# The second-last projection of a hybrid encoder layer: sixteen output columns one by one, or eight pairs by seven products with weight sums prepared earlier

## The chip, the cores and the metric

The kernel runs on one core of a Trainium2 chip. The metric is the device time of one execution in microseconds (us), lower is better. The core's engines run side by side and wait for each other through semaphores: TensorE (PE in the profile, its weight loads PEld), VectorE (DVE), ScalarE (ACT), GpSimd (POOL) and SyncE (SP), which here issues all the DMA transfers, from one queue, in order.

## The reference

One layer, 512 prompt tokens and 8x16 decode tokens, which the kernel handles as one block of T = 640 tokens, D = 2048:

```python
z = x @ w_in                                  # q, k, v, gates, merge gates
y_a = (fox_attention(q, k, v) * silu(gate_a)) @ w_out_fox
y_b = (rms_norm(gated_delta(...)) * silu(gate_b)) @ w_out_gdn
h = (sigmoid(m_a) * y_a + sigmoid(m_b) * y_b) @ w_out
x1 = layer_norm(DEEPNORM_ALPHA * x + h, ln_g, ln_b)
e = rms_norm(p_l @ w_pl_proj, pl_norm_w)
x_out = x1 + sigmoid(x1 @ w_pl_gate) * e
```

All in float32. The decode tokens' attention also reads a cache of 512 past rows for each of 8 heads. The change concerns `@ w_out` and what prepares it.

## The kernel before

**Products.** Every operand of a large product is split into a high and a low part (`xh`, `xl` of the activations; `wh`, `wl` of the weights): ACT casts the high part, DVE subtracts it from the source. Three matmuls (high by high, high by low, low by high) then stand for one product. Activations lie transposed, 16 tiles `k` of 128 features by 640 tokens, each in two halves of 320 tokens. One output column is 128 features: 16 steps `s`, each with 2 halves x 3 = 6 matmuls of 128x320, 96 in all, made by `column` (L319 and L320 in the profile). Its weights are two halves of 128x1024 (`wr`, three buffers, 512 KB each), cast in four pieces of 128x512 (L265 ACT, L266 DVE), up to five pieces ahead of their use (`w_ahead`; `plan` writes the list of halves and pieces).

**Pairs.** In the front, 14 pairs of columns go by seven products in place of eight (`pair`, L394): the 2x2 blocks (feature halves by column) of the weights are added and subtracted into seven combinations, the two token halves' activations into seven forms (X11, X21, X22, T1 to T4), and each product is 8 `k` by 3 matmuls. Sums of the products give both columns. There, the weight sums (b, S1, S2, S3) are made on DVE just ahead of their use (L255).

**Stages in order of time.** The front (input split, value columns, pairs) ends at about 505 us. Attention (`phase_fox`) follows to about 845 us: eight heads, each with a q and a k column of main matmuls, and between these the head's own work (scores, biases L622/L688, softmax L572 to L577, products with v) with loads of the k and v cache (`kc`, `vc`, four of 512 KB each). Then come the gated delta rule, w_out_fox, and `tail`: w_out_gdn to about 1778 us (eight double columns, each ending in `gated`, L1551 and L1554, which merges the branches into the tiles `mg`), w_out to about 2004 us (16 columns; L1625 adds `xr`, the input, giving the tile `r`; `moments`, L1588 to L1596, sums r and its square for the layer norm), and w_pl_gate on the split of r (`gsplit`, L305) to the end.

**What sets the order.** Nothing is scheduled by a compiler: the program's own order is each engine's order. Main matmuls are the beat; after every second step `tick` lets side work advance. Side work is generators in lanes (`work`, `conv`, ...), which yield the number of ticks to wait for (one tick is 0.88 us by the planner's clock); a dry lane may go on at every tick, the others at every second one and only with a free PSUM bank. The planner keeps an estimated clock of PE, DVE, ACT and POOL (`saw`), by which a positive yield also waits for the engines' work; it has none for DMA. `until(cond)` runs ticks with no matmuls until a condition holds.

**Tail.** The split of `mg[0..7]` stands in the w_out_gdn columns, of 8 to 11 in the last one's second half, of 12 to 15 in the first w_out column. `r[0..6]` are split in the last w_out column, the others in the first w_pl_gate column:

```python
            def after(s):
                if n == 15 and s >= 2 and s % 2 == 0:
                    gsplit(s // 2 - 1)
```

Tiles have their own names and buffers (`ld`, `m`, `re`, ...), and all 16 tiles r stay in SBUF.

## Time and profile before

| what | value |
|---|---|
| median of 3 runs | 2245.84 us (2243.6 to 2247.39) |
| the profiled execution's own time | 2244.35 us |
| its span | 2242.6 us |
| PE busy | 2230.1 us, 99% |
| DVE, ACT, POOL busy | 1332.7, 842.2, 68.5 us |
| granted TensorE clock | 0.999 |
| DMA | 304.56 MB, 136 GB/s over the span |

Times are microseconds from the start of the profiled span. The execution's own time has 1.75 us around the span. "L266" is line 266 of the program; `out<-in` names what an instruction writes and reads; "idle before, releaser" is the time the engine waited and for what. A DMA's "us to landing" counts from its issue on SP.

### The profile page before, as it was taken

The page shows a single profiled execution, that of the slowest core. Times are in us where ns is not written, and L with a number is a line of the kernel's source. Part 1 is how long each engine was busy: PE and PEld are TensorE (multiplying, and loading weights), DVE is VectorE, ACT ScalarE, POOL GpSimd, SP SyncE. Part 2 cuts the span into 40 slices and gives each one's busy share as a digit, 9 for nine tenths or more (in the row PEclk, how much of TensorE's full clock was granted, in tenths as well). Part 3 has the DMA queues.
Part 4 walks back from the last instruction along what each step waited for, and adds up shares of the span by engine and source line. Part 5 has one row for each costly group of instructions (what it writes and reads, how often), then busy time and mean ns, then how long its engine had stood idle before and what let it go on. Part 6 is the DMA issues. An engine that isn't in the chain of part 4 may idle for free.

```text
span 2242.6 us, 40023 instructions
## 1 busy us (share of the span) xinstructions
PE 2230.1 (99%) x15938; PEld 2160.2 (96%) x15938; DVE 1332.7 (59%) x2831; ACT 842.2 (38%) x1874; POOL 68.5 (3%) x230
## 2 busy tenths in 40 slices
PE   9999999999999999999999999999999999999999
PEld 7889999999999999999999999999999999999999
DVE  5476766663444445476686676686446534667555
ACT  4244444443333344443443543544332212242222
POOL 0000000000000000000000000000000000020000
PEclk9999999999999999999999999999999999999999
DMA  6333333238665634232332332335446522323332
GB/s 235 119 120 118 105 117 126 99 128 289 210 229 202 231 130 145 93 106 84 108 107 84 117 102 89 110 122 178 148 170 231 175 99 84 105 94 118 115 120 70
DMA packets 118378, 304.56 MB, mean 136 GB/s; under 512 B 22680, under 2 KB 30952, under 8 KB 118192
## 3 DMA queue, kind: packets, MB, share of 16 engines
q1 hardware_dynamic: 118192, 302.01, 40.3%
q8 instruction: 125, 2.05, 0.4%
q14 instruction: 61, 0.50, 0.1%
HBM read 250.15 MB, written 51.82 MB: 135 GB/s over the span
## 4 chain that ended last, share of the span: by engine, by line
PE 96%; DMA 2%; DVE 1%; ACT 0%; issue 0%; SPq 0%; DVEq 0%; ACTq 0%
PE g L319 34%; PE g L320 34%; PE g L394 15%; PE g L363 4%; PE s L363 1%; PE s L699 1%; DMA wr<-in_w 1%; PE s L657 1%; PE s L858 1%; PE s L616 1%; PE s L995 1%; DMA kc<-in_kc 0%; PE s L715 0%; PE s L1082 0%; PE s L1072 0%; PE s L1067 0%
## 5 line engine op out<-in xcount | busy, mean ns | idle before, releaser
L266 DVE TENSOR_TENSOR wl<-wr,wh 128x512 fp32r<-128x512 f32 x556 | 380.8, 690 | 523.2 <-ACT wh L265 516.3
L265 ACT CAST wh<-wr 128x512 fp32r<-128x512 f32 x556 | 342.5, 620 | 623.1 <-PE g L320 506.9
L319 PE MATMUL g<-xh,wh 128*128 128x320 f32 (+1 forms) x1712 | 549.6, 321 | 1.2 <-ACT wh L265 1.2
L319 PE MATMUL g<-xl,wh 128*128 128x320 f32 (+1 forms) x1712 | 529.9, 310 | 0.3 <-DVE xl L294 0.2
L320 PE MATMUL g<-xh,wh 128*128 128x320 f32 x1712 | 530.0, 310 | 0.0
L319 PE MATMUL g<-xh,wl 128*128 128x320 f32 (+1 forms) x1712 | 529.5, 309 | 0.0
L320 PE MATMUL g<-xl,wh 128*128 128x320 f32 x1712 | 529.5, 309 | 0.0
L320 PE MATMUL g<-xh,wl 128*128 128x320 f32 x1712 | 529.4, 309 | 0.0
L319 PEld LDWEIGHTS g<-xh,wh 128*128 128x128 f32 x1712 | 322.8, 189 | 14.1 <-issue 9.5
L320 PEld LDWEIGHTS g<-xh,wh 128*128 128x128 f32 x1712 | 322.7, 189 | 0.8
L319 PEld LDWEIGHTS g<-xl,wh 128*128 128x128 f32 x1712 | 322.5, 188 | 0.8 <-DVE xl L294 0.8
L319 PEld LDWEIGHTS g<-xh,wl 128*128 128x128 f32 x1712 | 322.0, 188 | 0.4 <-DVE wl L266 0.3
L320 PEld LDWEIGHTS g<-xl,wh 128*128 128x128 f32 x1712 | 322.3, 188 | 0.0
L320 PEld LDWEIGHTS g<-xh,wl 128*128 128x128 f32 x1712 | 322.1, 188 | 0.0
L394 PE MATMUL g<-xh,wh 128*128 128x320 f32 x448 | 138.6, 309 | 1.1 <-ACT u L404 1.1
L394 PE MATMUL g<-xh,wl 128*128 128x320 f32 x448 | 138.6, 309 | 0.0
L394 PE MATMUL g<-xl,wh 128*128 128x320 f32 x448 | 138.5, 309 | 0.0
L266 DVE TENSOR_TENSOR wl<-sr,wh 128x512 fp32r<-128x512 f32 x112 | 75.7, 690 | 62.3 <-ACT wh L265 62.0
L265 ACT CAST wh<-sr 128x512 fp32r<-128x512 f32 x112 | 67.8, 617 | 68.2 <-PE g L394 68.2
L394 PEld LDWEIGHTS g<-xh,wh 128*128 128x128 f32 x448 | 84.2, 188 | 1.4 <-ACT u L404 1.4
L394 PEld LDWEIGHTS g<-xh,wl 128*128 128x128 f32 x448 | 84.3, 188 | 0.0
L394 PEld LDWEIGHTS g<-xl,wh 128*128 128x128 f32 x448 | 84.1, 188 | 0.0
(388 smaller groups left out, 2918.4 us busy)
## 6 DMA issues: line engine op xcount, KB each, us to landing
wr<-in_w SPq DMA_DIRECT2D x276, 512.0 KB, 3.8
kc<-in_kc SPq DMA_DIRECT2D x32, 512.0 KB, 4.4
vc<-in_vc SPq DMA_DIRECT2D x32, 512.0 KB, 8.5
xr<-in_xT SPq DMA_DIRECT2D x32, 320.0 KB, 4.4
md<-m SPq DMA_DIRECT2D x32, 320.0 KB, 2.1
sab<-md SPq DMA_DIRECT2D x32, 320.0 KB
sr<-in_w SPq DMA_DIRECT2D x14, 512.0 KB, 3.6
ed<-e SPq DMA_DIRECT2D x16, 320.0 KB, 2.5
```

The source lines that it names most:

```text
L265: nc.scalar.copy(out=hi, in_=src)
L266: nc.vector.tensor_tensor(out=lo, in0=src, in1=hi.bitcast(F32), op=ALU.subtract)
L319: nc.tensor.matmul(ps[0], whl[w], xhl[o][:, a], start=(first and x == 0), stop=(last and x == 2))
L320: nc.tensor.matmul(ps[1], whl[w], xhl[o][:, b], start=(first and x == 0), stop=(last and x == 2))
L363: nc.tensor.matmul(ps, x[:, sl], w, start=(s == 0 and n == 0), stop=(s == 15 and n == 2))
L394: nc.tensor.matmul(ps, a[:, w], b, start=(k == 0 and n == 0 and not more), stop=(k == 7 and n == 2), skip_group_check=True)
L616: nc.tensor.matmul(s1[32 * j:32 * j + 32, :], self.qpad[:, 2 * j + par, :], kc[:, (j % 2) * NPT:(j % 2 + 1) * NPT], start=(par == 0), stop ...
L657: nc.tensor.matmul(od[32 * j:32 * j + 32, 0:P], self.ppad[:, c, 2 * j + par, :], vc[:, o:o + P], start=False, stop=(par == 1 and c == 3), ...
L699: nc.tensor.matmul(ops[:, 0:P], vn[:, kb, :], pT[:, kb * P:(kb + 1) * P], start=(kb == 0), stop=(kb == i))
L858: nc.tensor.matmul(pp[:, o:o + 256].rearrange("p (a b) -> p a b", a=2), hl[w][:, 0, x], hl[m][:, :, x], start=(n == 0), stop=(n == 2))
L995: nc.tensor.matmul(p[:, 0:2 * P].rearrange("p (a b) -> p a b", b=P), kt[g, 4, :], vm[g], start=True, stop=True)
```

## The change

The 16 columns of w_out become eight pairs by seven products, 168 matmuls of 128x320 for a pair in place of 192. Main matmuls in the whole program go from 13296 to 13104.

The four weight sums of each pair are made during attention by a new generator, `w_out_sums`, in a dry lane of its own: 16 iterations (eight pairs, two halves each), each with four loads of 256 KB (128x512: `b`, `d`, `a`, then `e`), four DVE operations and four stores to DRAM. The tiles `ws` have two buffers, so `e` reuses the buffer of `b` once b's sum is stored, and the next iteration's `b` and `a` reuse those of S2 and S3. All loads and stores are issued on SP. `after(12)` of the last attention column waits until the sums are done. In w_out each pair then loads seven halves (three from the weights, four sums) and casts 14 pieces.

In `tail` all tiles come from one list of 33 slots. The forms of `mg` are made during w_out_gdn and the first pair (`sums1`, `evens`, `odds`, `forms`). `fin` evacuates a pair. The tiles r[0..13] are stored to DRAM and loaded again during the last pair; `gsplit` 0 to 7 stand in the last two products of the last pair, 8 to 15 in the first gate column. The conv constants' load moves from ahead of attention to ahead of the gated delta rule; two merge columns use other buffers.

```diff
+        self.wsums, self.w0 = {}, n - 32
         while c < n:
+            if n - 32 <= c < n - 16:
+
+                for x in ("S1", "S2", "b", "S3"):
+                    self.wsums[c, x] = self.tc.dram_tile([P, 1024], F32, name=f"ws{c}{x}")
+                for i, key in enumerate(((c, 0), (c, "S2"), (c, 1), (c, "b"), (c, "S1"), (c + 1, 1), (c, "S3"))):
+                    self.halves.append((*key, "wr", 2))
+                    self.ops += [("p", key, p, ((c, i), p)) for p in range(2)]
+                c += 2
+                continue
...
+        src = self.wsums[half] if half in self.wsums else self.i["w"][2 * c + hf]
+        self.nc.sync.dma_start(out=self.raw[half][0][:, lo:hi], in_=src[:, lo:hi])
...
+    def w_out_sums(self):
+
+        nc = self.nc
+        op = nc.vector.tensor_tensor
+        for c in range(self.w0, self.w0 + 16, 2):
+            for p in range(2):
+                sl = slice(p * 512, p * 512 + 512)
+
+                def get(x, tag, bufs, hf):
+                    t = self.zt([P, 512 if tag == "ws" else T], tag, bufs, "ws")[:, 0:512]
+                    nc.sync.dma_start(out=t, in_=self.i["w"][2 * x + hf][:, sl])
+                    return t
+                b, d, a = get(c + 1, "ws", 2, 0), get(c + 1, "eacc", 1, 1), get(c, "ws", 2, 0)
+                yield 4
+                op(out=d, in0=b, in1=d, op=ALU.add)
+                op(out=b, in0=a, in1=b, op=ALU.subtract)
+                yield -2
+                nc.sync.dma_start(out=self.wsums[c, "S1"][:, sl], in_=d)
+                nc.sync.dma_start(out=self.wsums[c, "b"][:, sl], in_=b)
+                op(out=a, in0=d, in1=a, op=ALU.subtract)
+                yield -3
+                e = get(c, "ws", 2, 1)
+                nc.sync.dma_start(out=self.wsums[c, "S2"][:, sl], in_=a)
+                yield 4
+                op(out=e, in0=e, in1=a, op=ALU.subtract)
+                yield -2
+                nc.sync.dma_start(out=self.wsums[c, "S3"][:, sl], in_=e)
...
+        self.sums["gens"].append(self.w_out_sums())
...
-                self.until(lambda: min(self.qkdone) >= 7)
+                self.until(lambda: min(self.qkdone) >= 7 and not self.sums["gens"])
...
+        slots, where = deque(range(33)), {}
+
+        def new(dt=F32):
+            i = slots.popleft()
+            t = self.zp.tile([P, T], dt, tag=f"t{i}", name="t", bufs=1)
+            where[t.name] = i
+            return t
...
+        def form(name, k, x):
+
+            t = new(F32R)
+            hi, lo = t[:, a], t[:, b]
+            nc.scalar.copy(out=hi, in_=x)
+            tt(out=lo, in0=x, in1=hi.bitcast(F32), op=ALU.subtract)
+            xf[name][k] = hi, lo
+            return t
+
+        def sums1(k):
+            x, y = ab[k] = mg[2 * k], mg[2 * k + 1]
+            w = tw[k] = new()
+            tt(out=w[:, a], in0=x[:, b], in1=x[:, a], op=ALU.subtract)
+            tt(out=w[:, b], in0=y[:, b], in1=x[:, b], op=ALU.subtract)
+            tt(out=x[:, b], in0=w[:, b], in1=x[:, a], op=ALU.add)
+
+        def drop(k, x):
+
+            if (k, x) in held:
+                free(held.pop((k, x)))
+            else:
+                held[k, x] = ab[k][x]
...
+        def evens(k):
+            hi, lo = self.split(ab[k][0])
+            xf["X11"][k], xf["T2"][k] = (hi[:, a], lo[:, a]), (hi[:, b], lo[:, b])
+            drop(k, 0)
+
+        def odds(k):
+            hi, lo = self.split(ab[k][1])
+            xf["X21"][k], xf["X22"][k] = (hi[:, a], lo[:, a]), (hi[:, b], lo[:, b])
+            drop(k, 1)
...
-                if s % 8 == 5 and 1 <= n <= 8:
-                    nop[n - 1] = self.split(mg[n - 1])
+                k = u - 1
+                if k >= 0:
+                    if s == 2:
+                        sums1(k)
+                    if s == 12:
+                        evens(k)
+                    if k < 6:
+                        if s == 5:
+                            forms(k, "T3")
+                        if s == 7:
+                            forms(k, "T1")
+                        if s == 10:
+                            forms(k, "T4")
...
-                if u == 7 and s >= 8 and s % 2:
-                    k = 8 + (s - 9) // 2
-                    nop[k] = self.split(mg[k])
+                if u == 7 and s >= 9:
+                    odds(s - 9)
...
+            if n < 14:
+                nc.sync.dma_start(out=self.rr[n], in_=x)
+                free(x)
...
+        def fin(x, hf, z, p=None):
+            nonlocal acc1
+            n = 2 * m + x
+            o = r[n][:, (a, b)[hf]]
+            nc.vector.scalar_tensor_tensor(out=o, in0=o, scalar=2.0 * ALPHA, in1=z, op0=ALU.mult, op1=ALU.add)
+            if p is not None:
+                tt(out=o, in0=o, in1=p, op=ALU.add)
+            if m and (x, hf) in ((1, 0), (0, 1)):
+                moments(n)
+            if not m and (x, hf) == (0, 1):
+                acc1 = new()
+                tt(out=acc1, in0=r[0], in1=r[1], op=ALU.add)
...
-        for n in range(16):
-            def each(s):
-                if n == 0 and s < 4:
-                    nop[12 + s] = self.split(mg[12 + s])
...
-            def after(s):
-                if n == 15 and s >= 2 and s % 2 == 0:
-                    gsplit(s // 2 - 1)
...
+        first = deque([(0, 1, lambda: sums1(7)), (0, 3, lambda: evens(7)), (0, 5, lambda: odds(7)), (1, 0, lambda: forms(6, "T3")), (1, 2, lambda: forms(7, "T3")),
+                       (1, 4, lambda: forms(6, "T1")), (1, 6, lambda: forms(7, "T1")), (2, 2, lambda: forms(6, "T4")),
+                       (2, 4, lambda: forms(7, "T4"))])
+        for m in range(8):
+            def each(i, k):
+                nonlocal acc2, cmean
+                if m == 0:
+                    while first and first[0][:2] <= (i, k):
+                        first.popleft()[2]()
+                if (i, k) == (1, 0):
+                    xload(2 * m)
+                    xload(2 * m + 1)
+                if m == 1:
+                    if (i, k) == (0, 6):
+                        acc2, cmean = new(), new()
+                        for hf, sl in enumerate((a, b)):
+                            mp = self.sps()
+                            nc.tensor.matmul(mp[:, 0:HALF], self.ones, acc1[:, sl], start=True, stop=True)
+                            nc.scalar.mul(cmean[:, sl], mp[:, 0:HALF], 1.0 / 256)
+                    if (i, k) in ((1, 2), (1, 6)):
+                        moments(k // 4)
+
+                if m == 7 and i in (4, 5):
+                    free(tf.pop(("T3" if i == 4 else "T1", k)))
+                    j = k + 8 * (i - 4)
+                    if j < 14:
+                        r[j] = new()
+                        nc.sync.dma_start(out=r[j], in_=self.rr[j])
+                if m == 7 and i > 4 and k % 2 == 1:
+                    gsplit((i - 5) * 4 + k // 2)
+            self.pair(xf, fin, each, uv=(uv[:, a], uv[:, b]))
...
-                if n == 0 and s < 9:
-                    gsplit(7 + s)
+                if n == 0 and s < 8:
+                    gsplit(8 + s)
```

The engines' program order shows where the new work stands. First DVE at the start of head 0 of attention, around the q/k split (`ql`, `kl`) and up to the first bias (`xd`). Before:

```order
L266 TENSOR_TENSOR wl<-wr,wh 128x512 x3
L602 TENSOR_TENSOR ql<-q,qh 128x384
L602 TENSOR_TENSOR kl<-k,kh 128x512
L266 TENSOR_TENSOR wl<-wr,wh 128x512 x4
L622 SCALAR_TENSOR_TENSOR xd<-nbd,colT,s 128x512
L623 SCALAR_TENSOR_TENSOR xd<-nb,colT,s 128x128
L625 TENSOR_TENSOR xd<-xd,cb 128x128
L688 SCALAR_TENSOR_TENSOR xs<-nb,colT,s 128x128
L690 TENSOR_TENSOR xs<-xs,cb 128x128
```

Now (L305 is the `wl` subtraction, L265/L266 are S1 and b, L270 is S2, L275 is S3, L660 is the bias `xd`):

```order
L270 TENSOR_TENSOR ws<-ws 128x512
L305 TENSOR_TENSOR wl<-wr,wh 128x512
L640 TENSOR_TENSOR ql<-q,qh 128x384
L640 TENSOR_TENSOR kl<-k,kh 128x512
L305 TENSOR_TENSOR wl<-wr,wh 128x512
L275 TENSOR_TENSOR ws<-ws 128x512
L305 TENSOR_TENSOR wl<-wr,wh 128x512 x2
L265 TENSOR_TENSOR ws<-ws 128x512
L266 TENSOR_TENSOR ws<-ws 128x512
L270 TENSOR_TENSOR ws<-ws 128x512
L305 TENSOR_TENSOR wl<-wr,wh 128x512
L660 SCALAR_TENSOR_TENSOR xd<-nbd,colT,s 128x512
```

The first iteration's S1 and b stand right ahead of these rows. Its S2 and S3 and the next iteration's S1, b and S2 now stand among the `wl` and ahead of `xd`. SP at the same place, before:

```order
L551 DMA vc<-in_vc 128x1024 x4
L235 DMA wr<-in_w 128x1024
L591 DMA sg<-sgf_144 128x640
L557 DMA vn<-vd 128x5x128
L235 DMA wr<-in_w 128x1024 x2
L551 DMA kc<-in_kc 128x1024 x4
L235 DMA wr<-in_w 128x1024
L1333 DMA out_fk<-k 128x640
```

Now (`ws<-in_w` are loads of the sums' operands; `ws114S_170`, `ws114b`, `ws114S_171` and `ws114S_173` are the DRAM tiles of S1, b, S2 and S3):

```order
L589 DMA vc<-in_vc 128x1024 x4
L246 DMA wr<-in_w 128x1024
L268 DMA ws114S_170<-ws 128x512
L269 DMA ws114b<-ws 128x512
L629 DMA sg<-sgf_159 128x640
L595 DMA vn<-vd 128x5x128
L261 DMA ws<-in_w 128x512
L273 DMA ws114S_171<-ws 128x512
L246 DMA wr<-in_w 128x1024
L277 DMA ws114S_173<-ws 128x512
L261 DMA ws<-in_w 128x512 x3
L268 DMA ws114S_170<-ws 128x512
```

Two stores, the load of `e`, two more stores, the next three loads and two more stores now stand among the weight loads and the small loads; three loads of operands also stand ahead of the cache loads (`kc`, `vc`), above these rows.

DVE around the end of w_out_gdn, before (L1551 and L1554 are `gated`, L294 is the split's low half, L1625 the first evacuation of w_out):

```order
L294 TENSOR_TENSOR xl<-mg,xh 128x640
L1563 SCALAR_TENSOR_TENSOR sab<-sab 128x640
L294 TENSOR_TENSOR xl<-mg,xh 128x640
L266 TENSOR_TENSOR wl<-wr,wh 128x512
L294 TENSOR_TENSOR xl<-mg,xh 128x640 x2
L1551 SCALAR_TENSOR_TENSOR sab<-sab,g 128x320 x2
L1554 TENSOR_TENSOR mg<-sab 128x640
L294 TENSOR_TENSOR xl<-mg,xh 128x640
L266 TENSOR_TENSOR wl<-wr,wh 128x512
L294 TENSOR_TENSOR xl<-mg,xh 128x640 x3
L266 TENSOR_TENSOR wl<-wr,wh 128x512 x3
L1625 SCALAR_TENSOR_TENSOR r<-xr,g 128x320 x2
```

Now (L1602 and L1604 are `gated`, L333 is the split's low half, L1624 to L1626 are `sums1`):

```order
L333 TENSOR_TENSOR xl<-t,xh 128x640 x2
L1662 SCALAR_TENSOR_TENSOR t<-t 128x640
L333 TENSOR_TENSOR xl<-t,xh 128x640 x2
L305 TENSOR_TENSOR wl<-wr,wh 128x512
L333 TENSOR_TENSOR xl<-t,xh 128x640 x4
L1602 SCALAR_TENSOR_TENSOR t<-t,g 128x320 x2
L1604 TENSOR_TENSOR t<-t 128x640
L305 TENSOR_TENSOR wl<-wr,wh 128x512
L1624 TENSOR_TENSOR t<-t 128x320
L1625 TENSOR_TENSOR t<-t 128x320
L1626 TENSOR_TENSOR t<-t 128x320
L333 TENSOR_TENSOR xl<-t,xh 128x640
```

The splits that stood on both sides of the last `gated` now stand ahead of it, and the last tile's three sums and its split behind it.

DVE at the end of w_out, before (L1595 and L1596 are the last two operations of `moments`, L305 is `gsplit`):

```order
L1595 TENSOR_TENSOR acc_20009<-acc_20009,r 128x640
L1596 TENSOR_TENSOR acc_20010<-acc_20010,sq 128x640
L305 SCALAR_TENSOR_TENSOR xl<-r,cvec,xh 128x640
L266 TENSOR_TENSOR wl<-wr,wh 128x512
L305 SCALAR_TENSOR_TENSOR xl<-r,cvec,xh 128x640 x4
L266 TENSOR_TENSOR wl<-wr,wh 128x512
L305 SCALAR_TENSOR_TENSOR xl<-r,cvec,xh 128x640 x4
L266 TENSOR_TENSOR wl<-wr,wh 128x512
```

Now (L344 is `gsplit`, L1717 and L1719 are `fin`, L1699 to L1707 are `moments`):

```order
L344 SCALAR_TENSOR_TENSOR xl<-t,cvec,xh 128x640 x2
L305 TENSOR_TENSOR wl<-wr,wh 128x512
L344 SCALAR_TENSOR_TENSOR xl<-t,cvec,xh 128x640 x2
L1717 SCALAR_TENSOR_TENSOR t<-t,g 128x320
L1719 TENSOR_TENSOR t<-t 128x320
L1699 TENSOR_TENSOR t<-t 128x640
L1706 TENSOR_TENSOR t<-t 128x640
L1707 TENSOR_TENSOR t<-t 128x640
L344 SCALAR_TENSOR_TENSOR xl<-t,cvec,xh 128x640
L305 TENSOR_TENSOR wl<-wr,wh 128x512
L344 SCALAR_TENSOR_TENSOR xl<-t,cvec,xh 128x640 x4
L305 TENSOR_TENSOR wl<-wr,wh 128x512
```

The moments of two columns now stand between the splits of slots 0 to 7 and those of slots 8 to 15.

More of the change, by code (lines that the diff above doesn't have):

```diff
@@ L370, in wide, with pair @@
                 after(s)
-    def pair(self, xf, fin, each=None):
+    def pair(self, xf, fin, each=None, uv=None):
         nc = self.nc
@@ L1104, in run @@
         self.sqd = dr([P, T], F32, name="sqd")
+        self.red = dr([P, T], F32, name="red")
+        self.rr = [dr([P, T], F32, name=f"rr{i}") for i in range(14)]
         self.sgd = [dr([P, T], F32, name=f"sgd{i}") for i in range(H)]
@@ L1115, in run @@
         work, conv, self.ends = self.lane(), self.lane(True), self.lane()
-        self.blocks, self.chunks = self.lane(True), self.lane()
+        self.blocks, self.chunks, self.sums = self.lane(True), self.lane(), self.lane(True)
         self.work = work
@@ L1121, in run @@
                     self.front(work)
-                c2 = ctx.enter_context(tc.tile_pool(name="cs2", bufs=1))
+                with tc.tile_pool(name="zf", bufs=1) as self.zp:
+                    self.phase_fox(work)
+            with tc.tile_pool(name="ps2g", bufs=4, space=bass.MemoryType.PSUM) as self.ps2, \
+                    tc.tile_pool(name="cs2", bufs=1) as c2, tc.tile_pool(name="zg", bufs=1) as self.zp:
                 self.cvst = c2.tile([P, 24, 24], F32, name="cvst")
@@ L1334, in phase_fox @@
             work["gens"].append(head(h, *qk))
-        for _ in range(2):
-            self.mcol("eacc")
+        self.mcol("sg", 2)
+        self.mcol("vn", 2)
         op, pr = [], []
@@ L1635, in tail @@
+        for x in (uv, *tf.values()):
+            free(x)
         self.op = gop
         self.cut = slice(0, HALF + 2), slice(HALF + 2, T + 2)
-        rs = self.zt([P, T], "rs")
-        nmd, el = cmean, {}
+        rs, nmd, re, el = new(), cmean, new(), {}
+        nc.sync.dma_start(out=re, in_=self.red)
         def norm():
@@ L1788, in _layout @@
         bl += [np.concatenate([wo[2 * i], wo[2 * i + 1]], 1) for i in range(8)]
-    bl += list(_wblock(a["w_out"][0]))
+    for b in _wblock(a["w_out"][0]):
+        bl.append(b.reshape(P, KT // 2, 2, P).transpose(0, 2, 1, 3).reshape(P, DM))
     bl += list(_wblock(a["w_pl_gate"][0]))
```

98 lines of the change are left out of this document (44 added, 54 removed).

## The prediction

> **What bounds the kernel now.** The page comes first: the head, the busy times, the chain.
>
> ```profile
> span 2242.6 us, 40023 instructions
> PE 2230.1 (99%) x15938; PEld 2160.2 (96%) x15938; DVE 1332.7 (59%) x2831; ACT 842.2 (38%) x1874; POOL 68.5 (3%) x230
> PE 96%; DMA 2%; DVE 1%; ACT 0%; issue 0%; SPq 0%; DVEq 0%; ACTq 0%
> PE g L319 34%; PE g L320 34%; PE g L394 15%; PE g L363 4%; PE s L363 1%; PE s L699 1%; DMA wr<-in_w 1%; PE s L657 1%; PE s L858 1%; PE s L616 1%; PE s L995 1%; DMA kc<-in_kc 0%; PE s L715 0%; PE s L1082 0%; PE s L1072 0%; PE s L1067 0%
> ```
>
> TensorE (PE) carries 96% of the chain and is idle for 2242.6 - 2230.1 = 12.5 us. So a matmul that goes takes its time with it, and whatever makes PE wait adds its whole length. The windows then show each stage the change touches (columns: PE, weight loads, DVE, ACT, POOL, granted clock, DMA share, GB/s).
>
> ```profile
> 520.00:540.00 20.00, 17.03 (x112) 15.15 (x111) 7.57 (x19) 4.16 (x11) 0.47 (x2) 0.91 1.01 379
> 580.00:620.00 40.00, 40.00 (x386) 37.59 (x385) 18.28 (x46) 14.09 (x35) 0.47 (x2) 1.00 0.65 212
> 1778.00:1792.00 14.00, 14.00 (x98) 14.00 (x97) 7.16 (x11) 4.32 (x8) 0.00 (x0) 1.00 0.39 132
> 1800.00:1850.00 50.00, 50.00 (x342) 50.00 (x341) 15.66 (x26) 8.70 (x14) 0.00 (x0) 1.00 0.30 101
> 2000.00:2050.00 50.00, 50.00 (x341) 48.91 (x340) 39.18 (x66) 21.36 (x34) 4.95 (x18) 1.00 0.31 102
> ```
>
> PE is never idle at the start (1778), in the middle and at the end (2000) of the w_out stage, nor in a steady attention head (580 to 620). It is idle in the first head (520 to 540), where the DMA engines are full at 379 GB/s. PE's table of waits has one entry of more than 1.2 us, the idle time in this window, and the chain says what led to it (start, length, what).
>
> ```profile
> PE s L715 <- DVE xs L577: 3.0, 1, 3.0
> 162.68 336.87 PE g L394 x2292
> 508.31 0.43 SPq L235
> 509.99 9.24 DMA kc<-in_kc
> 519.30 10.19 DMA wr<-in_w
> 529.58 0.63 ACT wh L265
> 530.85 0.74 DVE xd L622
> 537.04 0.47 PE s L715
> ```
>
> A weight load issued at 519.30 behind the cache loads lands 10.19 us later. Its cast and `wl` stand on DVE ahead of the head's first bias `xd`, and PE waits for the softmax that follows until 537.04.
>
> **The gain.** The front's pairs ran 2292 matmuls in 336.87 us, 0.147 us each; the window from 1800 agrees (342 in 50 us). Two columns are 192 matmuls, a pair of seven products 7x8x3 = 168. Eight pairs save 8x24 = 192, and 192x0.147 = **28.2 us**, all on the path. Everything else in the change can only give this back; the prices follow from these rows (mean ns; DMA: KB, us to landing).
>
> ```profile
> L266 DVE TENSOR_TENSOR wl<-wr,wh 128x512 fp32r<-128x512 f32 x556 | 380.8, 690 | 523.2 <-ACT wh L265 516.3 <-DMA lanes<-ld 2.3 <-DMA nb<-rd 1.8
> L1551 DVE SCALAR_TENSOR_TENSOR sab<-sab,g 128x320 f32<-128x320 f32 x32 | 14.1, 483 | 23.2 <-PE g L319 23.2
> L1595 DVE TENSOR_TENSOR acc<-acc,r 128x640 f32<-128x640 f32 x15 | 12.4, 825 | 0.5
> wr<-in_w SPq DMA_DIRECT2D x276, 512.0 KB, 3.8
> vc<-in_vc SPq DMA_DIRECT2D x32, 512.0 KB, 8.5
> md<-m SPq DMA_DIRECT2D x32, 320.0 KB, 2.1
> L622 DVE SCALAR_TENSOR_TENSOR xd<-nbd,colT,s x8: 743/748/748, 530.8 to 791.3; 128x512 f32<-128x512 f32 x8
> DVE xd L622 <- PE s L616: 26.9, 7, 4.5
> ```
>
> **The sums in throughput: nothing.** Sixteen iterations with four DVE operations of 128x512 are 64x0.69 = 44 us. A head lasts (791.3 - 530.8)/7 = 37.2 us with DVE busy 18.28 of 40; two iterations a head add 5.5. Their 128 transfers of 256 KB are 33.6 MB; from 508 to 791, where the order puts the last of them, that is 119 GB/s beside 212, together 331 of the 379 seen. The cover is this bandwidth; without it each MB costs 2.6 us.
>
> **The sums in head 0: +13 us.** DVE now has `e` (L275) and the next iteration's first three sums ahead of `xd`; SP has three loads ahead of the cache loads. Step by step: three loads at 379 GB/s shift the queue by 2.1 us, so the weight load of 519.30 lands at 531.6. The store of `b` lies behind it and lands at about 532.3. Only then may `e`'s load be issued, since it takes `b`'s buffer; 3.8 us for it give 536.1, and 0.69 on DVE 536.8. S3's store (2.1, as `md`) lands at 538.9; the next `a` reuses `e`'s buffer, so its load starts there and lands at 542.7. Two sums and one `wl` (2.1 us) put `xd` at 544.8, 13.9 us later than 530.85. If 256 KB land in 2.8 us and not in the 3.8 of 512 KB, it is 11.9. PE has the same work between the scores and L715 in both orders, so this is idle time: 13 us taken, 8 to 16 kept (less if the store passes the cache loads, more if the wait on SP also holds the weights behind it). SP stands at `e`'s load with a weight load, S2's and S3's stores behind it; these are in the chain already.
>
> The Trainium skill, "DMA: Bandwidth & Descriptors", section on rules for kernel authors, says to issue a DMA early and to wait for it late; by that rule the sums, which wait a few microseconds after each issue, should stall in every head and not in this one alone. That result is the slower rival below. The trace agrees so far as its own loads, issued well ahead, stall PE only in head 0.
>
> **The sums in heads 1 to 7: +3 us.** One iteration is a ring: `b` store 2.1, `e` load 3.8, sum 0.69, S3 store 2.1, next `a` load 3.8, two sums 1.4: 13.9 us. Sixteen of them in 283 us have 17.7 each. DVE waits for PE before `xd` by 26.9/7 = 3.8 us a head, so it can be late by that much. I take 3 us for head 1, which starts late, and for odd cases; bounds 0 and the rival's 39.
>
> **The start of w_out: +6.1 us.** The queue on DVE in these rows gives the spacing.
>
> ```profile
> 1780.92 2.29 DVE L294 TENSOR_TENSOR xl<-mg,xh 128x640 fp32r<-128x640 f32 x3
> 537.04 0.47 PE L715 MATMUL s<-cb,xs 128*128 128x128 f32 x1 [2.97 <-DVE xs L577]
> 538.53 0.47 PE L320 MATMUL g<-xh,wh 128*128 128x320 f32 x1
> 538.80 0.47 PE L319 MATMUL g<-xl,wh 128*128 128x320 f32 x1
> 539.83 0.31 PE L319 MATMUL g<-xh,wh 128*128 128x320 f32 x1
> 539.98 0.31 PE L320 MATMUL g<-xh,wh 128*128 128x320 f32 x1
> ```
>
> A split is 2.29/3 = 0.76. Before, four splits stood in the last w_out_gdn column and four in the first of w_out, in its `s` order, and PE never waited. Now eight stand in the second half of the last column. From its middle, 7.05 us (48 matmuls) before its end, DVE has `gated` 1.64 (2x0.45 and 0.75), two `wl` 1.2, eight splits 6.1, a gate 0.75: 9.7, so it is 2.6 late at the end. Then `gated` 1.64, `wl` 0.6, three sums of half a tile 1.3, the cast and the split of `evens(7)` 1.5, and some hand-overs 0.3: X11 of the last k is there 7.9 us after the column's end. PE comes for it after 21 matmuls, at 3.1: a stall of 4.8 (bounds 3 and 6). After an idle time of 2.97 us matmuls stood 0.27 apart until 539.83, then 0.15: about ten at nearly twice the time, 1.3 us. The same is added here; in head 0 before has it already.
>
> The Trainium skill, "TensorE: Matmul & The Clock Gate", part on the two states, has the clock fall to half after an idle window of about 3.4 us and rise after as long a busy one. The trace differs a little: 2.97 us were enough. By the page the recovery would cost an estimated 1.7 us in place of 1.3.
>
> **The end of w_out: +3.4 us.** Of this stretch, before:
>
> ```profile
> 2004.70 0.89 DVE L1625 SCALAR_TENSOR_TENSOR r<-xr,g 128x320 f32<-128x320 f32 x2 [0.56 <-PE g L319]
> 2005.62 0.83 DVE L1588 TENSOR_TENSOR r<-r,cm 128x640 f32<-128x640 f32 x1
> 2013.19 3.27 DVE L305 SCALAR_TENSOR_TENSOR xl<-r,cvec,xh 128x640 fp32r<-128x640 f32 x4
> 2016.38 0.68 DVE L266 TENSOR_TENSOR wl<-wr,wh 128x512 fp32r<-128x512 f32 x1
> ```
>
> One `gsplit` is 3.27/4 = 0.82. Seven were spread over the last column, nine over the gate's first, ended at 2016.4, and PE was busy for 50.00 of 50. Now eight stand in products 5 and 6 of the last pair, with `fin` and the moments of two columns behind them: 6.5 + four `wl` 2.6 + `fin` 1.9 + six moment operations 4.9 = 15.9 us of DVE from product 5 on, and then the split of slot 8, 16.8. PE comes for slot 8 at 7.06 + 7.06 = 14.1: 2.7 us, and DVE's 0.82 a split with a `wl` among four does not gain on PE's 0.88 a step: 0.7 more. Bounds 2 and 5.
>
> **At nothing.** Weights: seven halves a pair in 24.7 us are 149 GB/s, and attention ran at 212. Cover: five pieces ahead. The pair's DVE work (14 `wl`, 9.7 us, adds and moments, some 8) is 18 of 24.7. The stores and reloads of `rr` are 28 x 320 KB = 9.2 MB; the reloads sit in products 4 and 5, each a product (3.5 us) ahead of its split, against 2.1 for a store and 3.8 for a load of 512 KB. Cover: that product; without it 1 us or so. The conv constants' load moves off head 0's SP queue: 0.4 us, taken as nothing.
>
> **Sum.** Against the profiled run's own 2244.35 us (1.5 below the median 2245.84): -28.2 + 13 + 3 + 6.1 + 3.4 = -2.7, so 2241.7; on the median's scale 2243.1. Changes within 0.2% (4.5 us) cannot be told from none.
>
> **The rivals.**
> *A, the forecast*: most of the gain comes back in three waits. 0.44; its own range 2236 to 2252.
> *B, the waits are smaller*: head 0 stalls by 8, the start by 3, the end by 2, the heads not at all: -15.2, 2231. For it: head 0's queue may drain faster than 379 GB/s bounds it. Against: the ring's two landings in a row are in program order. 0.20. Its floor, no waits, is 2217.6.
> *C, every head waits*: one landing like `vc`'s 8.5 in place of 3.8 adds 4.7, just over the ring's 17.7 - 13.9 = 3.8. In head 0 both landings are like that; if one iteration in each of seven heads has two, it is late by 9.4 - 3.8 = 5.6, 39 in all: 2279. It decides for slower from about 10 us, 0.7 in each of 14 iterations. For it: each head issues four `vc` and four `kc` on the same queue, and SP waits in order. Against: DVE's 3.8 us of waiting before `xd`, and a DMA share of 0.65. 0.28.
> *D, w_out's pairs don't run at PE's pace*: seven loads and not four, from two sources. If one landing of 3.8 us shows in each of eight pairs, 30 us: 2273, and the change has not brought what it says. For it: nothing but the number of loads. Against: five pieces ahead, 149 of the 379 GB/s. 0.08.
>
> **Numbers.** A gives 2243. Range 2228 to 2268: it leaves out B's lowest part and C's and D's upper part. Faster: B and 0.14 of A, 0.34; same: 0.25 of A; slower: C, D and 0.05 of A, 0.41.
>
> **What would show it.** Right: 13104 main matmuls; pairs of w_out in 24.7 us with PE full; one PE wait of some 16 us in head 0 (xs), one of 5 at the start of w_out (a split of `evens`), one or several of 3 in the gate's first column. Wrong: waits for xs in each head (C), idle PE inside the pairs with a wait for `wh` (D), no wait over 8 us in head 0 (B), or PE waits elsewhere that nothing here names.

## The result and the profile after

The changed kernel takes 2280.78 us (median of 4 runs, 2279.83 to 2285.34), the kernel before 2246.61 us (4 runs): 1.0157 times as long, 95% interval 1.0139 to 1.0176. The profiled execution took 2281.4 us. It is slower by 34 us, outside the stated range; the time is that of rival C (2279).

The page's head, the busy times and the chain:

```profile
span 2279.6 us, 40353 instructions
PE 2217.2 (97%) x15746; PEld 2141.7 (94%) x15746; DVE 1437.3 (63%) x3032; ACT 878.9 (39%) x1954; POOL 69.3 (3%) x230
PE 85%; DMA 10%; DVE 3%; issue 1%; ACT 1%; SPq 1%; DVEq 0%; ACTq 0%
PE g L358 25%; PE g L359 24%; PE g L432 23%; DMA ws<-in_w 4%; PE g L402 4%; PE s L402 1%; DMA ws118b<-ws 1%; DVE wl L305 1%; DMA ws122b<-ws 1%; PE s L896 1%; PE s L695 1%; DMA ws116S<-ws 1%; DMA ws114b<-ws 0%; PE s L1033 0%; DMA kc<-in_kc 0
```

PE is idle for 62.4 us in place of 12.5, and busy for only 12.9 us less where 28.2 us of matmuls went. Its granted clock fell from 0.999 to 0.991 of the span, and to 0.65 between 540 and 560 us, so I read the difference of 15.3 us as matmuls that ran slower after waits (the last section shows some). On the chain stand now the loads and stores of the sums (`ws`).

Where along the program it goes is read from three marks, of before and then of after: the first bias of each head, the merge at the end of w_out_gdn's columns, the first copy of each gate column (first and last start, us).

```profile
L1551 DVE SCALAR_TENSOR_TENSOR sab<-sab,g x32: 478/481/489, 1674.0 to 1778.3; 128x320 f32<-128x320 f32 x32
L1669 DVE COPY gb<-g x16: 151/151/159, 2034.0 to 2231.8; 128x2 f32<-128x2 f32 x16
```

```profile
L660 DVE SCALAR_TENSOR_TENSOR xd<-nbd,colT,s x8: 736/741/746, 543.0 to 845.1; 128x512 f32<-128x512 f32 x8
L1602 DVE SCALAR_TENSOR_TENSOR t<-t,g x32: 476/482/489, 1727.5 to 1835.1; 128x320 f32<-128x320 f32 x32
L1798 DVE COPY gb<-g x16: 150/152/159, 2071.4 to 2268.7; 128x2 f32<-128x2 f32 x16
```

| stretch | lateness at its end | share of the stretch | predicted |
|---|---|---|---|
| attention, head 0 (xd, 530.8 before) | 12.2 | +12.2 | +13 |
| heads 1 to 7 (xd, 791.3 before) | 53.8 | **+41.6** | **+3** |
| to the first `gated` | 53.5 | -0.3 | 0 |
| w_out with its start and end, to the last gate column | 36.9 | -16.6 | -18.7 |

PE's table of waits names the places:

```profile
PE s L753 <- DVE xs L615: 34.7, 12, 10.5
PE s L673 <- DVE xd L615: 5.1, 3, 2.3
PE g L358 <- DVE wl L305: 3.7, 1, 3.7
PE g L432 <- ACT xh L332: 3.7, 1, 3.7
PE g L358 <- ACT xh L343: 2.3, 1, 2.3
```

At L753 and L673 PE needs the softmax's results, for which it now waits 12 and 3 times, where before there was one wait of 3.0 us. The 3.7 us for a `wl` at L358 is in head 0; the 3.7 us at L432 is the start of w_out, the 2.3 us for an `xh` at L358 its end. What DVE waited for during attention:

```profile
DVE ws L275 <- DMA ws<-in_w: 78.0, 13, 16.9
DVE wl L305 <- ACT wh L304: 43.5, 32, 2.5
DVE ws L265 <- DMA ws<-in_w: 23.4, 10, 4.8
DVE ws L266 <- DMA ws<-in_w: 10.1, 10, 2.2
```

DVE stood 78 us at S3 (L275), whose operand `e` hadn't landed, and 33.5 us at S1 and b. The chain shows a whole round in head 2 (start, length, what):

```profile
609.72 8.48 DMA ws118b<-ws
618.21 3.33 DMA ws<-in_w
621.63 0.62 DVE ws L275
622.35 2.62 DMA ws118S<-ws
624.99 3.92 DMA ws<-in_w
628.99 0.69 DVE ws L266
629.68 0.30 DVE xd L660
629.98 5.54 DMA ws118b<-ws
```

These are the steps of the predicted ring, store, load, sum, store, load, sum, and the head's `xd` right behind on DVE. This round takes 20.3 us, not 13.9: the store of `b` needs 8.48 us in place of 2.1. SP's list shows what stood ahead of it: the four `vc` loads (2 MB).

```profile
607.02 1.76 SPq L589 DMA_DIRECT2D vc<-in_vc  x4
608.88 0.75 SPq L268 DMA_DIRECT2D ws118S<-ws  x1
609.72 0.39 SPq L269 DMA_DIRECT2D ws118b<-ws  x1
618.21 0.33 SPq L261 DMA_DIRECT2D ws<-in_w  x1
```

It is not the store of `b` as such. Five transfers of the sums on the chain (256 KB each, stores and loads) were issued right behind four `vc` loads and took 8.2 to 10.1 us; S3's stores, where no such loads were issued just ahead, took 2.0 to 3.0.

Over all, the sums go from the first load at 507.6 us to the last S3 at 848.5 us: 21.3 us an iteration. Before, a head lasted 37.2 us, which leaves 18.6 for each of its two iterations. PE waits for what can't keep up.

### The profile page after: what moved, and what is told of

The parts are those of the page before. It is cut to its first block, busy times and chain, and to the rows that moved or that the text cites. A ratio compares the mean times of both kernels' runs of the same rounds, so it can differ in the third digit from the quotient of the medians.

```text
span 2279.6 us, 40353 instructions
## 1 busy us (share of the span) xinstructions
PE 2217.2 (97%) x15746; PEld 2141.7 (94%) x15746; DVE 1437.3 (63%) x3032; ACT 878.9 (39%) x1954; POOL 69.3 (3%) x230
## 4 chain that ended last, share of the span: by engine, by line
PE 85%; DMA 10%; DVE 3%; issue 1%; ACT 1%; SPq 1%; DVEq 0%; ACTq 0%
PE g L358 25%; PE g L359 24%; PE g L432 23%; DMA ws<-in_w 4%; PE g L402 4%; PE s L402 1%; DMA ws118b<-ws 1%; DVE wl L305 1%; DMA ws122b<-ws 1%; PE s L896 1%; PE s L695 1%; DMA ws116S<-ws 1%; DMA ws114b<-ws 0%; PE s L1033 0%; DMA kc<-in_kc 0%
## 5 line engine op out<-in xcount | busy, mean ns | idle before, releaser
L305 DVE TENSOR_TENSOR wl<-wr,wh 128x512 fp32r<-128x512 f32 x604 | 411.0, 689 | 409.0 <-ACT wh L304 405.8
L304 ACT CAST wh<-wr 128x512 fp32r<-128x512 f32 x604 | 369.8, 620 | 546.5 <-PE g L359 352.4
L358 PE MATMUL g<-xh,wh 128*128 128x320 f32 (+1 forms) x1456 | 471.8, 324 | 3.4 <-ACT xh L343 2.3
L358 PE MATMUL g<-xh,wl 128*128 128x320 f32 (+1 forms) x1456 | 452.0, 310 | 3.7 <-DVE wl L305 3.7
L358 PE MATMUL g<-xl,wh 128*128 128x320 f32 (+1 forms) x1456 | 452.6, 311 | 1.0 <-DVE xl L344 0.7
L358 PEld LDWEIGHTS g<-xh,wh 128*128 128x128 f32 x1456 | 275.9, 190 | 16.5 <-issue 12.1
L358 PEld LDWEIGHTS g<-xh,wl 128*128 128x128 f32 x1456 | 275.2, 189 | 4.2 <-DVE wl L305 4.0
L358 PEld LDWEIGHTS g<-xl,wh 128*128 128x128 f32 x1456 | 275.7, 189 | 2.0 <-issue 1.1
L359 PEld LDWEIGHTS g<-xh,wh 128*128 128x128 f32 x1456 | 275.9, 189 | 0.7
L359 PEld LDWEIGHTS g<-xl,wh 128*128 128x128 f32 x1456 | 275.5, 189 | 0.0
L359 PEld LDWEIGHTS g<-xh,wl 128*128 128x128 f32 x1456 | 275.1, 189 | 0.0
L432 PE MATMUL g<-xh,wh 128*128 128x320 f32 x704 | 218.8, 311 | 4.8 <-ACT xh L332 3.7
L432 PE MATMUL g<-xl,wh 128*128 128x320 f32 x704 | 218.3, 310 | 0.4 <-DVE xl L333 0.4
L432 PE MATMUL g<-xh,wl 128*128 128x320 f32 x704 | 218.5, 310 | 0.0
L432 PEld LDWEIGHTS g<-xh,wh 128*128 128x128 f32 x704 | 132.9, 189 | 5.5 <-ACT xh L332 3.9
L432 PE MATMUL g<-t,wh 128*128 128x320 f32 x608 | 134.1, 309 | 0.0
L432 PEld LDWEIGHTS g<-xl,wh 128*128 128x128 f32 x704 | 132.9, 189 | 0.8 <-DVE xl L333 0.7
L432 PEld LDWEIGHTS g<-xh,wl 128*128 128x128 f32 x704 | 133.1, 189 | 0.0
L305 DVE TENSOR_TENSOR wl<-sr,wh 128x512 fp32r<-128x512 f32 x112 | 75.7, 690 | 62.3 <-ACT wh L304 62.1
```

Source lines behind the costliest of these rows:

```text
L304: nc.scalar.copy(out=hi, in_=src)
L305: nc.vector.tensor_tensor(out=lo, in0=src, in1=hi.bitcast(F32), op=ALU.subtract)
L358: nc.tensor.matmul(ps[0], whl[w], xhl[o][:, a], start=(first and x == 0), stop=(last and x == 2))
L359: nc.tensor.matmul(ps[1], whl[w], xhl[o][:, b], start=(first and x == 0), stop=(last and x == 2))
L432: nc.tensor.matmul(ps, a[:, w], b, start=(k == 0 and n == 0 and not more), stop=(k == 7 and n == 2), skip_group_check=True)
```

## The experiments

The theory that the runs test: the cost is made by engines that work in order. DVE, and SP, stand at a sum's operand whose load waits for a store behind bulk loads, and a head's own work stands behind them; two landings and two stores in a row in each iteration are longer than its share of attention. Rival 1: the 33.6 MB of traffic delay attention's own loads. Rival 2: the 44 us of sums are too much for DVE. Ratios are to the kernel before, with the 95% interval.

**The sums left out** (their four halves are replaced by other halves of the weights):

```diff
-        src = self.wsums[half] if half in self.wsums else self.i["w"][2 * c + hf]
+        src = self.i["w"][2 * c + (hf if half not in self.wsums else {"S2": 1, "b": 2, "S1": 3, "S3": 0}[hf])]
...
-        self.sums["gens"].append(self.w_out_sums())
...
-                self.until(lambda: min(self.qkdone) >= 7 and not self.sums["gens"])
+                self.until(lambda: min(self.qkdone) >= 7)
```

> The sums during attention are left out altogether (no loads, no operations on DVE, no stores); the pairs of w_out load other halves of the weights in the place of the sums, so the values of w_out are not the reference's, its instructions and transfers are. All theories put the cost in attention, so attention should be as before the change, and the time 2246.6 - 28.2 + some 10 (the two waits around w_out, 4.1 and 3.0 us, and the slow matmuls after each): about 2228. If it stays above 2245, the pairs themselves are slow.

Measured: 2226.39 us, 0.9911 (0.9896 to 0.9926). So the sums cost 54.4 us, and the rest of the change brings 2226.4 - 2245.7 = -19.3: the 28.2 us of matmuls less 8.9, where the forecast for the start and the end of w_out was 9.5. Attention is as before here: the biases run from 530.5 to 791.2 us, PE waits for the softmax once (2.8 us).

**The sums on POOL:**

```diff
-        op = nc.vector.tensor_tensor
+        op = nc.gpsimd.tensor_tensor
```

> The four operations of the sums go from DVE to POOL; loads, stores and their waits on SP stay. Theory (ring and order: DVE stands in program order at a sum whose operand is not there, with the softmax behind it): only POOL waits now, and about 45 of the 53 us that attention lost come back, 2230 to 2240. Rival 1 (the 33.6 MB of traffic delay attention's own loads): no change, 2275 to 2285. Rival 2 (44 us more work on DVE is too much): like the theory, 2230 to 2240; the next run tells these two apart.

Measured: 2295.53 us, 1.0219 (1.0202 to 1.0236): slower still, which no theory had. PE's and POOL's waits in that run:

```profile
PE s L654 <- POOL qpad L633: 47.9, 7, 14.1
POOL ws L275 <- DMA ws<-in_w: 137.9, 15, 16.9
POOL ws L265 <- DMA ws<-in_w: 97.6, 14, 14.9
```

The wait moved with the sums: each head makes two copies on POOL (`qpad`, L633), and these now stood behind the waiting sums. DVE's waits at the sums are gone, and so is rival 2 as the whole cause.

**The same, with the head's two `qpad` copies on DVE:**

```diff
-        op = nc.vector.tensor_tensor
+        op = nc.gpsimd.tensor_tensor
...
-            nc.gpsimd.tensor_copy(   # qpad
+            nc.vector.tensor_copy(   # qpad
```

> As e2 (sums on POOL), and the two copies of each head that stood behind them on POOL (L633, qpad) go to DVE; nothing of a head's chain is left on the engine that waits for the sums' loads. Theory (what costs is an engine that stands, in order, with the head's chain behind it): PE's 47.9 us of waiting at L654 go, and the time is 2232 to 2250; what is left is SP, which stands at the same waits with cache and weight loads behind it. Rival 1 (traffic): same transfers, no change against e2, 2285 to 2300.

Measured: 2285.1 us, 1.0174 (1.0154 to 1.0195). The 47.9 us are gone, but the time is not where the theory had it. PE, DVE, ACT and SP wait as follows:

```profile
PE s L737 <- DMA vn<-vd: 23.6, 6, 6.6
DVE xd L660 <- DMA nbd<-sfd: 35.7, 6, 10.4
ACT wh L304 <- DMA wr<-in_w: 30.0, 7, 13.8
SPq L277 <- POOL ws L275: 56.7, 14, 8.6
SPq L268 <- POOL ws L265: 24.3, 14, 3.2
```

Now attention's own loads are late: SP stands at the stores of the sums (56.7 and 24.3 us) with `nbd`, `vn` and weight loads behind them. The theory held for DVE alone; SP, which issues everything, is the second engine that passes the wait on. I had given what is left 6 to 24 us (2232 to 2250 against e1's 2226); 59 stayed. The time also lies at the lower edge of what rival 1 gave (2285 to 2300), so this run alone does not speak against the traffic; the one with all loads together, below, does.

**Four ws tiles** (no load waits for a store of the iteration before), with its control, since the room comes from `PIECES`:

```diff
-    PIECES = 5
+    PIECES = 4
...
-                b, d, a = get(c + 1, "ws", 2, 0), ..., get(c, "ws", 2, 0)
+                b, d, a = get(c + 1, "ws", 4, 0), ..., get(c, "ws", 4, 0)
...
-                e = get(c, "ws", 2, 1)
+                e = get(c, "ws", 4, 1)
```

> Four ws tiles in place of two, so that no load of the sums waits for a store of the iteration before it; to make room there are four pieces of cast weights ahead in place of five (next run). The sums stay on DVE, with the same traffic. Theory: the store falls out of the way from one sum to the next, the load stays; of 53 us about half come back, 2250 to 2262, and DVE's waits at L275 fall from 78 us to under 40. Rival 1 and rival 2 (same traffic, same work on DVE): no change, 2275 to 2290.

> Only the room for run e3: four pieces of cast weights ahead in place of five, two ws tiles. All theories: within 5 us of the changed kernel, 2276 to 2290. If it is slower by more, e3 has to be read against this run.

Measured: 2269.92 us, 1.0106 (1.0086 to 1.0126), and the control 2285.02 us, 1.0173 (1.0153 to 1.0194). The stores in the ring are worth 15 us, less than the expected half. DVE still waited 65.4 us at L275: `e`'s load is issued behind the stores of S1 and b, for which SP has to wait until DVE has made them, so two landings in a row are left.

**All four loads together** (four tiles, four pieces; the operations follow ten ticks later, the stores after them; new lines only, shortened):

```diff
+                b, d = get(c + 1, "ws", 4, 0), get(c + 1, "eacc", 1, 1)
+                a, e = get(c, "ws", 4, 0), get(c, "ws", 4, 1)
+                yield 10
                 op(...)  # S1, b, S2, S3 in a row
                 yield -3
                 # four stores
+                yield 3
```

> Sums on DVE in attention, four ws tiles and four pieces ahead as in e3; all four loads of an iteration are issued together, ten ticks (8.8 us by the planner's clock) ahead of the four operations, which follow each other, and the four stores after them. No load waits for a store of its own iteration, and DVE has one place to wait in an iteration. Same traffic and same DVE work as e3. Theory: DVE's waits for the sums fall from e3's 98 us to under 30, 2240 to 2256. Rival 1 and rival 2: as e3, 2270.

Measured: 2240.56 us, 0.9976 (0.9966 to 0.9987). Against the control with the same pieces, 44 us came back with the same traffic and the same work on DVE, and DVE's waits for the sums' loads fell from e3's 97.9 us to 16.1. That rules out rivals 1 and 2 as the cause of these 44 us. Of the 54.4 us, 14 are left against e1, some 4 of them the control's; how the others divide is open.

**The lead of the loads** (against the run before):

```diff
-                yield 10
+                yield 4
...
-                yield 3
+                yield 9
```

> e6 with one number changed: the four operations follow their loads after four ticks (3.5 us by the planner's clock) and not ten; the six ticks are added behind the stores, so that the pace is the same. Theory: a load that lands in 3 to 8 us behind the cache and weight loads is then not there when DVE comes to it, in most of 16 iterations; DVE's waits for the sums' loads rise from e6's 16 us to 40 or more, and of e6's gain 10 to 25 us are lost, 2250 to 2265. If only the stores in the ring cost, and not the lead of the loads: as e6, 2240.

Measured: 2242.94 us, 0.9988 (0.9978 to 0.9999): 2.4 us more than e6, not the 10 to 25 that were expected. Head 0 has a wait of 12.9 us, where e6 had 8.2; the windows of heads 1 to 7 are full:

```profile
580.00:620.00 40.00, 40.00 (x336) 37.90 (x335) 23.86 (x53) 13.10 (x32) 0.47 (x2) 1.00 0.90 322
620.00:660.00 40.00, 40.00 (x336) 37.91 (x335) 23.83 (x52) 13.73 (x33) 0.47 (x2) 1.00 0.92 326
660.00:700.00 40.00, 40.00 (x338) 37.42 (x341) 23.62 (x51) 13.10 (x32) 0.47 (x2) 1.00 0.90 329
```

PE is busy for 40.00 of 40 us at 322 to 329 GB/s and a DMA share of 0.9; the changed kernel had 271 to 309 GB/s in these 120 us with PE idle for 15 of them. But the lead did not become as short as the edit was to make it. From the issue of an iteration's first load to its first sum the trace has, in head 2 for example:

```profile
593.17 2.34 SPq L261 DMA_DIRECT2D ws<-in_w  x4
601.18 0.68 DVE L266 TENSOR_TENSOR ws<-ws 128x512 f32<-128x512 f32 x1
```

That is 8.0 us; from the third iteration on it is 6.6 to 10.4 us in e9 and 8.9 to 15.3 in e6, and those of the sums' transfers in e9 whose landing the trace has took 2.6 to 8.9 us from their issue (median 5.1). So a lead of some 8 us was enough in heads 1 to 7. A lead shorter than most landings was not tested there, and head 0's longer wait speaks for the lead having its price where the queue is full.

e3 and e9 have the same tiles, pieces and traffic, and e9 is 27 us faster. It has one landing in an iteration where e3 has two (`e`'s load is issued only when S1 and b are made, and S3 waits for it at once), and all its stores stand behind all its operations. The runs don't say how the 27 us divide between the second landing, its missing lead and SP's standing at the stores.

**A later start** of the sums, nothing else:

```diff
+        yield 16
         for c in range(self.w0, self.w0 + 16, 2):
```

> The changed kernel with one number: the sums start 16 ticks later, so that their first loads go behind head 0's cache loads and only S1, b and S2 of the first iteration stand ahead of head 0's first bias. Theory (two landings and two stores in a row in each iteration, behind bulk loads, longer than an iteration's share of attention): head 0 gains some 8 us, the other heads go on losing 35 to 40: 2268 to 2276. If head 0's lateness is what all the later heads carry along, most of the 54 us goes: 2230 to 2245.

Measured: 2273.25 us, 1.0123 (1.0104 to 1.0141), in the theory's range. The heads' biases run from 537.2 to 836.8 us:

```profile
L661 DVE SCALAR_TENSOR_TENSOR xd<-nbd,colT,s x8: 737/742/746, 537.2 to 836.8; 128x512 f32<-128x512 f32 x8
```

Head 0 is 5.8 us earlier, and the other seven lose 299.6 - 260.5 = 39.1 us, where the changed kernel lost 41.6. Head 0's lateness isn't what they carry along.

**The sums in the gated delta rule** (quarters of 128x256 and four pieces for room), and the same with splits and moments around w_out moved:

```diff
-        self.sums["gens"].append(self.w_out_sums())     # phase_fox
...
+        self.sums["gens"].append(self.w_out_sums())     # phase_gdn
...
# only in the second run, e8:
-                    odds(s - 9)                         # s >= 9
+                    odds((s - 9) // 2)                  # s = 9, 11, 13, 15; the other four in the first products
...
+                if n == 0 and s in (9, 11):
+                    late.pop()()                        # acc1, acc2 of columns 14 and 15
```

> The generator of e6 in the gated delta rule stage and not in attention; for room in quarters of 128x256, 32 iterations, four pieces ahead. Attention is free of the sums; the DMA engines are busy for 0.2 to 0.3 of the new stage and 0.63 of attention before. Theory: landings are quick there, no waits over 2 us from the sums, 2228 to 2238 (e1's 2226 and the 4 us of e4). Rival 2 (DVE work): DVE is busier in this stage than in attention, so the same work costs as much, 2260 or more.

> e7, and the two waits around w_out taken on: four of the eight odd splits go from the end of w_out_gdn into the first products of w_out, and the two accumulations of the last two columns' moments (L1706, L1707) go behind the splits of the first gate column. If the two waits are as read (4.1 us and 3.0 us, with about 1.3 us of slow matmuls after each), this is 6 to 10 us faster than e7: 2220 to 2230. If other work takes their place on DVE, it is the same as e7.

Measured: 2254.38 us, 1.0034 (1.0022 to 1.0045), and 2256.07 us, 1.0043 (1.0028 to 1.0058). In e8 one of the moved accumulations stands behind the layer norm's sums, so y is not the reference's there. e7 missed its forecast by 16 us: DVE waited only 1.6 us for the sums' loads, and still PE waits for the recurrence on DVE (first and third row) and for a load of its own (`st`, 6.2 us; 0.8 in e1):

```profile
PE s L1101 <- DVE rp L1097: 6.7, 3, 2.8
PE s L1001 <- DMA st<-in_st: 6.2, 2, 5.1
PE s L1093 <- DVE S L1111: 4.3, 3, 3.0
```

There rival 2 has its share, and the `st` row speaks for rival 1; how the 24 us (2254.4 - 2226.4 less the 4 of the control) divide is open. In e8, which was to be 6 to 10 us faster than e7, the wait at the start of w_out fell from 3.7 to 1.5 us, and a wait of 4.9 us of the layer norm's sums for the moved moments took the saving back.

**All together**: e6's grouping, a start 16 ticks later, the moved splits, and of the last two moments all but the subtraction behind `gsplit` 15. First with ten ticks of lead and the layer norm's sums at tick 12, then with six ticks of lead that don't heed the planner's estimate, and tick 18 (the second against the first):

```diff
-                yield 10
+                yield -6
...
-                yield 2
+                yield 7
...
-            yield 12       # norm()
+            yield 18
```

> e6 with the sums starting 16 ticks later, behind head 0's cache loads (2 ticks less behind each iteration's stores); four of the eight odd splits in the first products of w_out (as e8); and of the last two columns' moments all but the subtraction behind the splits of the first gate column, with the layer norm's own sums two ticks later. Theory: head 0's 8.2 us wait goes back to about 3 (5 us), the wait at the start of w_out from 3.9 to under 2 with fewer slow matmuls (3 us), that at its end from 3.1 to about 1 (2 to 3 us): 2229 to 2234. If other work takes a wait's place, up to 2240.

> As e10 (four loads together, start 16 ticks later, splits and moments around w_out moved), with the operations six ticks behind the loads whatever the planner's estimate of DVE says, seven ticks behind the stores (the heads then stand in the program where they stood in e9), and the layer norm's own sums six ticks later still. Theory: e10's idle time at the end of attention (5 us) and its wait for the moments (4.0 us) go: 2228 to 2233. If the moments' wait only moves on to the first evacuation of the gate, 2233 to 2237.

Measured: 2238.04 us, 0.9967 (0.9955 to 0.9979), then 2232.45 us, 0.9940 (0.9926 to 0.9953). The first lost 4.0 us at the layer norm's sums (L1539) and 5.5 us of idle PE at the end of attention, where the planner had pushed head 7 behind the last main matmuls. The second has neither:

```profile
PE s L750 <- DVE xs L612: 10.0, 2, 8.3
PE g L429 <- ACT wh L301: 2.5, 1, 2.5
PE g L429 <- ACT xh L329: 1.5, 1, 1.5
```

It beats both kernels, by 13 us and 48 us. Left are 8.3 us in head 0, though the sums start 16 ticks later here too, and 2.5 us at the front's first pair (L429), a wait that the runs with four pieces have and the changed kernel has not. With the same start and ten ticks of lead (the first of the two) PE's wait for the softmax in head 0 was 1.4 us. That too speaks for the lead in head 0, though the two runs differ in more than this.

## Why the prediction was wrong

**What failed: "The sums in heads 1 to 7: +3 us".** Measured, +41.6. The mechanism stood in that paragraph, the ring of store, load, sum, store, load, sum; the size of its terms was wrong. I took medians over the whole kernel, of other transfers (2.1 for a store of 320 KB, 3.8 for a load of 512 KB), 13.9 us against 17.7. In the round shown the store of `b` took 8.48 us, which alone makes it 20.3; in the mean an iteration took 21.3. Only the first ring, in head 0, took what was predicted: 13.98 us from S3 at 535.07 to S3 at 549.05. The prediction had the right duration in a row already, `vc`'s 8.5 us to landing behind its own kind, used it for head 0, and left it to the rival for the others.

The cover I named, DVE's 3.8 us of waiting before each `xd`, was real and was used up: DVE waited for PE there for 26.9 us before and for 3.2 after. It does not help once the ring is the slower of the two, since two rounds of 21.3 us are 42.6 where a head lasted 37.2: 5.4 us in each of seven heads, 38 of the 41.6. The share of 17.7 was a little short itself (18.6 by the 37.2 us of a head).

**Rival C**, "every head waits", gave two long landings in one iteration of each head, 13.9 + 9.4 = 23.3 us, 39 in all, 2279. Measured: 41.6 and 2280.8, with `vc` ahead of the sums' transfer. In heads 2 to 5 the iterations with `vc` took 22.0 to 24.3 us from S3 to S3, the others 18.8 to 19.6, which is near what a head leaves them. It should have been the forecast. In its parts it fits less well: such an iteration on the chain has one transfer of 8.2 to 10.1 us and not two landings of 8.5, so that the total came so near is partly luck. The argument against it, a DMA share of 0.65, was a mean over the stage; the long transfers stand right behind 2 MB of loads.

**The rule to issue early and wait late** (the Trainium skill, "DMA: Bandwidth & Descriptors", rules for kernel authors) spoke for rival C, and the changed kernel agrees: PE waited 15 times at the softmax. So does e9, where an iteration's loads are issued 6.6 us and more ahead of their first use: its windows of heads 1 to 7 have PE full. No run here shows a shorter lead than that in these heads with all the loads together.

**Right, by their own terms.** The gain: 13104 main matmuls, PE full inside the pairs, e1's -19.3 against -18.7. Head 0: `xd` 12.2 us late against 13, by the predicted steps: `e`'s load was issued at 531.82 (forecast 532.3), and the next `a` was there for DVE at 541.07 (forecast 542.7), as the chain of after has it.

```profile
522.98 8.82 DMA ws114b<-ws
531.82 3.13 DMA ws<-in_w
541.07 0.70 DVE ws L266
```

Its idle time came in two pieces, 3.7 us for a `wl` behind S3 and 10.5 for the softmax. The start of w_out: 3.7 + 0.4 us of waiting against 4.8 (a sum that took 0.6 us for a `wl` whose row has 0.69). Its end: 2.3 + 0.7 us against 3.4. Throughput at nothing: 331 GB/s forecast, 322 to 329 measured in e9 with PE full. Rival D did not come: no wait for a weight inside the pairs of w_out.

**Against A as a whole**: three waits did take back most of the gain, as it says; the fourth, priced at 3, took more than all of it.

## What to carry to other kernels

Price a transfer by what is issued right ahead of it on its queue, not by its median: here 256 KB took 2.0 to 3.0 us (S3's stores, with no such loads just ahead) and, right behind 2 MB of loads, 8.2 to 10.1. Work that is free in throughput still costs when several landings follow each other in one iteration; count the landings and stores in a row, compare their sum with the iteration's share of the stage, and issue all loads together, ahead of their use by more than a landing, and all stores at the end. Moving such work to an idle engine moved the wait here to what shared that engine, and then to the queue that issued for it.

## What the runs showed of the hardware that I had not expected

The sums of 128x512 took 0.69 us on DVE and 1.29 to 1.39 us on POOL, by groups of e2:

```profile
L266 POOL TENSOR_TENSOR ws<-ws 128x512 f32<-128x512 f32 x16 | 22.2, 1388 | 5.0 <-DMA ws<-in_w 2.7 <-issue 1.1 <-POOL ws L265 0.2
L265 POOL TENSOR_TENSOR ws<-ws 128x512 f32<-128x512 f32 x16 | 20.7, 1291 | 111.7 <-DMA ws<-in_w 97.6 <-issue 14.2
```

After the 10.5 us of idle time in head 0 matmuls stood 0.27 us apart from 549.2 to 554.2, for 5 us; after 2.97 us of idle time before the change it was 2.8 us.

```profile
549.19 0.47 PE L753 MATMUL s<-cb,xs 128*128 128x128 f32 x1 [10.52 <-DVE xs L615]
550.42 0.47 PE L358 MATMUL g<-xh,wh 128*128 128x320 f32 x1
553.36 0.47 PE L359 MATMUL g<-xh,wl 128*128 128x320 f32 x1
554.41 0.31 PE L359 MATMUL g<-xh,wh 128*128 128x320 f32 x1
```

The Trainium skill, "TensorE: Matmul & The Clock Gate", part on the two states, has about 3.4 us of busy time for the way back; both values here, 2.8 and 5, lie around it, and in a kernel with 15 such waits at the softmax they add up: PE's busy time fell by 12.9 us where 28.2 us of matmuls went, and slow matmuls are my reading of the 15.3 us between. In e1, with the same 15746 matmuls and no sums, PE was busy for 2206.3 us in place of 2217.2: 10.9 of the 15.3 us came with the sums' waits.
